# Down-projection of an encoder layer: where the lower weight parts of the odd pieces are made

## The chip, the cores and the metric

The kernel runs on one core of a Trainium2 chip. The metric is the time on the device in microseconds, the median of the timed runs. TensorE multiplies matrices out of SBUF into PSUM; VectorE, ScalarE and GpSimd work on elements; SyncE issues the plain loads from HBM, and GpSimd has a queue of transfers of its own. All transfers run on the same 16 DMA engines.

## The reference

One layer of an encoder for 256 tokens of width 2048: a mixer (forgetting attention and HGRN2), a cross attention, and a gated feed-forward block with a causal convolution, each followed by a residual and a layer norm. The change touches only the last product, `w_down`:

```
def conv_ffn(x, w_up, conv_w, conv_b, w_down):
    h = x @ w_up
    ...
    a, b = jnp.split(h, 2, axis=-1)
    return (jax.nn.silu(a) * b) @ w_down
...
ff = conv_ffn(x, ffn_up[l], conv_w[l], conv_b[l], ffn_down[l])
x = layer_norm(DEEPNORM_ALPHA * x + ff, ln3_g[l], ln3_b[l])
```

The inner width is 5632, so `w_down` is 5632 x 2048. Everything is float32.

## The kernel before

All products run in float32r, the reduced float32 of TensorE. To keep the precision each operand is split into two parts: the upper part is the value rounded to float32r, and the lower part is what the rounding left, value minus upper part. `split` (lines 76 to 78) does it with two instructions: ScalarE casts the raw tile to the upper part, VectorE subtracts the upper part from the raw tile. A product then takes three matmuls: upper activation by upper weight, upper by lower, and lower by upper (`tok_steps`, lines 256 to 258).

Weights come in pieces of 128 partitions by 2048 columns, 1 MB, one `Load` each. `Load.dma` asks SyncE for the piece into a ring of three raw tiles (`RAW_BUFS`). `Load.split` makes, for each half of 1024 columns, a tile `whi` and a tile `wlo` of 4 KB a partition, out of a pool of 38 such tiles (`unit`) that the activations and other data share. A raw tile is free again when both halves are split, and a `whi` or `wlo` tile when TensorE has used it for the last time.

The program is a list of slots. For each slot `run` first calls `advance`, which traces the loads and splits of the pieces that lie ahead (one piece of splits and three of loads, in the down-projection), then the slot's matmuls. The order on each engine's queue follows from that; how early an instruction really runs is set by the tiles that it waits for.

The down-projection is the last `block_output` (line 1071): the 2048 output columns in four chunks of 512, for each chunk 11 pieces of four k-tiles (44 in all), and for each piece `tok_steps` for both blocks of 128 tokens: 24 matmuls of 128x512. In the last chunk the last four pieces share a slot, first for the one token block and then for the other (`stagger=4`). After the second chunk `load_gb` fetches the parameters of the last norm into four more tiles of the shared pool. Behind the last matmul come the residual, the statistics, the norm and the stores.

Of the kernel before, what the change touches and what calls it, by code (L numbers as in the profile page):

```python
# [38 lines left out]
# the second norm's hand-over to the feed-forward products, by (token block, chunk, half of the chunk)  # L39
# [5 lines left out]
def tile_encoder_layer(ctx: ExitStack, tc: tile.TileContext, aps, out):  # L45
# [8 lines left out]
    def unit(shape, dtype=F32, name="u"):  # L54
        """4 KB a partition, from the pool that all larger data share."""
        return up.tile(shape, dtype, name=name, tag="u", bufs=UNITS)
# [13 lines left out]
    def hold(inst, after):  # L70
        """Keeps an instruction without operands, and its tile, from being scheduled before another."""
        tc.add_manual_dep(inst.ins, after.ins.name, mybir.DependencyInfo(
            mybir.DependencyClass.NoSync, mybir.DependencyReason.DATA), reason="hold")

# [13 lines left out]
    class Load:  # L88
        """One [128, 2048] piece of weights (or of a transposed activation)."""

        def __init__(self, src, into=None):
            self.src, self.into = src, into
# [8 lines left out]
        def split(self):  # L101
            if self.into is not None:
                split_act(self.into, r3(self.raw, 8), 0, 8)
                return
            self.halves = []
            for h in range(2):
                hi = unit([P, 1024], F32R, name="whi")
                lo = unit([P, 1024], F32R, name="wlo")
                split(hi, lo, self.raw[:, h * 1024:(h + 1) * 1024])
                self.halves.append((hi, lo))  # L110

    def fetch(dst, src):
        """A smaller load, queued behind the weights that have been asked for."""
        hold(nc.sync.dma_start(dst, src), state["load"])
# [15 lines left out]
    def background(make):  # L130
        """make() gives a generator; each slot runs its next step."""
        program.append(("bg", make))
# [9 lines left out]
    def later(fn, slots=1):  # L142
        """Traces fn some slots on, when the engines no longer wait for what it needs."""
        deferred.setdefault(state["slot"] + slots, []).append(fn)
# [9 lines left out]
    def advance(dma_to, split_to):  # L154
        """Asks for weights as far as their ring of tiles reaches, and splits them."""
        while True:
            while state["dma"] < min(dma_to, state["split"] + RAW_BUFS, len(loads)):
                loads[state["dma"]].dma(2 if state["dma"] == 2 else 1)
                state["dma"] += 1
            if state["split"] >= min(split_to, len(loads)):  # L160
                return
            loads[state["split"]].split()
            state["split"] += 1
# [29 lines left out]
    def ft_steps(acc, halves, act, k0=0, k1=KD):  # L193
        """[128 features, 512]: the two halves add up to the product for 256 tokens."""
        for k in range(k0, k1):
            hi, lo = halves[k // 8]
            cols = slice((k % 8) * P, (k % 8) * P + P)
            x = k_of(act, k)
            nc.tensor.matmul(acc, lhsT=hi[:, cols], rhs=flat(x), start=k == 0, stop=False)  # L199
            nc.tensor.matmul(acc[:, 0:S], lhsT=lo[:, cols], rhs=x[:, 0], start=False, stop=k == KD - 1)  # L200

    def block_steps(acc, halves, act, k0, k1, t):
        """One matmul alone starts the bank: the second block's first ones find it cleared."""
        ts = slice(t * P, t * P + P)
        for k in range(k0, k1):
            hi, lo = halves[k // 8]
            cols = slice((k % 8) * P, (k % 8) * P + P)
            x = k_of(act, k)
            nc.tensor.matmul(r3(acc, 2)[:, :, ts], lhsT=hi[:, cols], rhs=x[:, :, ts],  # L209
                             start=k == 0 and t == 0, stop=False)  # L210
            if t == 1:
                nc.tensor.matmul(acc[:, 0:S], lhsT=lo[:, cols], rhs=x[:, 0], start=False, stop=k == KD - 1)  # L212
# [15 lines left out]
    def products(srcs, act, evacs, steps=None):  # L228
        """Several of them, four k-tiles of each at a time. With steps, the second half of the tokens
        comes after the first, and the products with the lower parts of the weights come with it."""  # L230
        acc = []

        def body(*halves):
            acc.extend(bank("acc", "g") for _ in halves)
            for t in range(2 if steps else 1):
                for c in range(4):
                    for i, h in enumerate(halves):
                        if steps:
                            steps(t, c, i)
                            block_steps(acc[i], h, act, 4 * c, 4 * c + 4, t)  # L240
                        else:
                            ft_steps(acc[i], h, act, 4 * c, 4 * c + 4)

        def post():
            for a, evac in zip(acc, evacs):
                evac(a)

        slot(srcs, body, post, ahead=0 if steps else None)
# [11 lines left out]
    def product_tok(srcs, act, evac, order=None, stagger=0, between=None, inside=None):  # L260
        """Two [128 tokens, 512 columns] products; srcs: pieces of four k-tiles. evac(t, product)"""
# [48 lines left out]
    def keep_warm(n):  # L310
        """Products of nothing, for the clock of the tensor engine while it waits."""
        b = bank("warm", "m")
        for i in range(n):
            nc.tensor.matmul(b, lhsT=idle, rhs=idle.unsqueeze(1).broadcast_to((P, 4, P)), start=True, stop=True)

    def start():
        """The first operands, piece by piece, so that the products start early."""
# [31 lines left out]
    def parameters():  # L349
# [15 lines left out]
        # lower bound of the forget gate: softmax over a depth of one, less its first row  # L365
# [9 lines left out]
    def rsqrt(v, shape, name):  # L375
        """v ** -0.5: a guess from the exponent, then three Newton steps y <- (v y y - 3 c c) y. Each
        takes c times the root to -2 c c c times it; the guess has the c that ends at one."""
# [48 lines left out]
    def hgrn(g, d):  # L426
# [5 lines left out]
        # gates  # L432
# [13 lines left out]
        # products of gates within blocks of four: up to t (pre), after s (suf)  # L446
# [16 lines left out]
        # blocks of eight, referred to their middle  # L463
# [36 lines left out]
        def upper(t, h):  # L500
            """The upper halves of blocks of 2 h."""
            return t.rearrange("p (n i) -> p n i", i=2 * h)[:, :, h:2 * h]

        a = level(dk, dq)
        # from here on q and k carry the products within their block of h
# [54 lines left out]
        # outputs in token layout, RMS norm, gate  # L560
# [55 lines left out]
    def forget_bias():  # L616
# [9 lines left out]
        # log sigmoid  # L626
# [9 lines left out]
        # running sum over tokens  # L636
# [143 lines left out]
    def block_output(w, pieces, act, n, ln, after=None, order=None, stagger=3, inside=None, affine=True):  # L780
        """Adds act @ w to the residual; n gets the norm's parameters by token block, and its g and b."""
# [17 lines left out]
        for c in range(4):  # L799
            product_tok([w[pieces * c + i] for i in range(pieces)], act, evac(c), order,  # L800
                        stagger=stagger if c == 3 else 0, inside=inside if c == 3 else None)
            if c == 1 and affine:
                then(load_gb)

    def norm_transposed(n, act):
        """Normalises and lays all out transposed, four k-tiles a step."""
# [20 lines left out]
    def standardise(n, c, t):  # L827
        """The norm without its g and b."""
# [4 lines left out]
    def block_transposed(act, c, t):  # L833
        """Four k-tiles of a standardised token block, transposed; the steps given put g and b in, and split."""
# [24 lines left out]
    def affine(ln):  # L859
        """g and b for a residual that is standardised."""  # L860
# [14 lines left out]
    def feature_into(d, h, j):  # L875
        """Features of a head, split; d[h][j // 2][:, j % 2, part]"""
# [153 lines left out]
    def inside(left):  # L1030
        """The first token block, laid out transposed among the last products of the second."""
        if left == 1:
            transpose(0, 0, 1, 2, 3)
            advance_chunks(0, 0, 1, 0, 1, 2, 2, 3, 3)

    def norm_steps(t, c, i):
        """The second block, among the products of the first and its own."""
# [37 lines left out]
def _by_feature(w):  # L1075
    """[K, F] -> [F / 128, 128, (K / 128) * 128]"""
# [4 lines left out]
def _by_column(w):  # L1081
    """[K, C] -> [(C / 512) * (K / 512), 128, 4 * 512]"""
# [58 lines left out]
```

## Time and profile before

| | |
|---|---|
| median of 2 timed runs | 1587.66 us (1587.35 to 1587.98) |
| span of the profiled execution | 1586.8 us, at a mean granted clock of 0.997 |
| TensorE busy | 1570.9 us, 99% of the span |
| VectorE busy | 1023.3 us, 64% |
| ScalarE busy | 772.5 us, 49% |
| GpSimd busy | 10.9 us, 1% |
| moved by the DMA engines | 299.29 MB, 189 GB/s in the mean |

Only the profiled execution has a span, from its first instruction to its last; the timed runs are other executions, and their median is 0.9 us above it. Busy times overlap, so they don't add up to the span. Times of rows count from the start of the span; the matmuls of the down-projection lie between 1334 and 1574 us.

### The profile page before, as it was taken

Reading aid. Unit: us, or ns where it says so; the run is one execution under the profiler, and the core shown is the slowest. Engines: PE = TensorE matmul, PEld = TensorE weight load, DVE = VectorE, ACT = ScalarE, POOL = GpSimd, SP = SyncE. Lnnn points to the kernel's source line nnn. Section 1 sums busy time; section 2 is a strip of 40 time slices with the busy share of each in tenths; the row PEclk is TensorE's granted clock in tenths of the full one; section 3 lists DMA queues with packets and bytes.
Section 4 is the critical chain, followed back from the end, with each engine's and each line's share of the span. In section 5 each row is a group of like instructions: output and inputs, shape, how many; then the busy total and the mean of one; then the engine's idle time right before and its main releaser. Section 6 shows DMA issues by size and latency. Waiting matters only on the chain.

```text
span 1586.8 us, 20787 instructions
## 1 busy us (share of the span) xinstructions
PE 1570.9 (99%) x8324; PEld 1343.6 (85%) x8324; DVE 1023.3 (64%) x1444; ACT 772.5 (49%) x1128; POOL 10.9 (1%) x24
## 2 busy tenths in 40 slices
PE   9999999999999999999999999999999999999996
PEld 7888888888888888888889888888888888888885
DVE  6567468667664765554847976676766667454464
ACT  5453354455553344443627655565555555343350
POOL 0000000000000000000000000000000000000000
PEclk9999999999999999999999999999999999999999
DMA  8555255455446544445733754554454556556551
GB/s 306 188 229 226 108 195 184 179 219 199 157 176 223 201 178 167 159 160 185 269 129 133 267 206 164 213 185 166 179 182 164 182 177 226 196 200 212 189 208 54
DMA packets 45793, 299.29 MB, mean 189 GB/s; under 512 B 5368, under 2 KB 5760, under 8 KB 11264
## 3 DMA queue, kind: packets, MB, share of 16 engines
q1 hardware_dynamic: 45376, 296.90, 51.1%
q8 instruction: 65, 1.06, 0.3%
q0 software_dynamic: 320, 1.06, 0.2%
q14 instruction: 32, 0.26, 0.0%
HBM read 295.83 MB, written 2.11 MB: 188 GB/s over the span
## 4 chain that ended last, share of the span: by engine, by line
PE 98%; DVE 1%; DMA 0%; issue 0%; SPq 0%; DVEq 0%; ACT 0%
PE acc L199 35%; PE acc L200 18%; PE acc L256 13%; PE acc L258 13%; PE acc L257 13%; PE xs L903 1%; PE xo L933 1%; PE lev L526 1%; PE acc L209 0%; PE acc L212 0%; DMA xraw<-in_xT_dram 0%; PE fo L750 0%; PE ntr L838 0%; PE ffacc L613 0%; PE ho L568 0%; PE lev L492 0%
## 5 line engine op out<-in xcount | busy, mean ns | idle before, releaser
L199 PE MATMUL acc<-act,whi 128*128 128x512 f32 x2384 | 844.1, 399 | 1.5 <-DVE act L78 1.4
L78 DVE TENSOR_TENSOR wlo<-raw,whi 128x1024 fp32r<-128x1024 f32 (+1 forms) x540 | 642.0, 1213 | 261.6 <-ACT whi L77 232.6
L77 ACT CAST whi<-raw 128x1024 fp32r<-128x1024 f32 (+1 forms) x540 | 547.8, 1044 | 262.6 <-PE acc L257 184.1
L200 PE MATMUL acc<-act,wlo 128*128 128x256 f32 x2384 | 669.2, 281 | 0.2 <-DVE wlo L78 0.2
L199 PEld LDWEIGHTS acc<-act,whi 128*128 128x128 f32 x2384 | 448.5, 188 | 111.9 <-DVE act L78 1.7
L200 PEld LDWEIGHTS acc<-act,wlo 128*128 128x128 f32 x2384 | 450.8, 189 | 0.8 <-DVE wlo L78 0.5
L256 PE MATMUL acc<-whi,act 128*128 128x512 f32 x800 | 312.7, 391 | 0.0
L258 PE MATMUL acc<-whi,act 128*128 128x512 f32 x800 | 311.5, 389 | 0.0
L257 PE MATMUL acc<-wlo,act 128*128 128x512 f32 x800 | 311.3, 389 | 0.0
L258 PEld LDWEIGHTS acc<-whi,act 128*128 128x128 f32 x800 | 150.1, 188 | 31.6
L256 PEld LDWEIGHTS acc<-whi,act 128*128 128x128 f32 x800 | 150.2, 188 | 30.6
L257 PEld LDWEIGHTS acc<-wlo,act 128*128 128x128 f32 x800 | 150.2, 188 | 30.5
L216 ACT COPY half<-acc 128x256 f32<-128x256 f32 x144 | 53.2, 370 | 165.2 <-PE acc L200 164.7
L949 ACT ACTIVATE cy<-hbuf,convp 128x256 f32<-128x256 f32 x88 | 52.9, 601 | 45.0 <-DVE hbuf L217 44.4
L950 DVE SCALAR_TENSOR_TENSOR cy<-hbuf,convp,cy 128x256 f32<-128x256 f32 x88 | 42.4, 483 | 38.9 <-ACT cy L949 38.9
L77 ACT CAST act<-cy 128x256 fp32r<-128x256 f32 x76 | 30.9, 407 | 56.4 <-DVE cy L968 43.3
L217 DVE TENSOR_TENSOR hbuf<-acc,half 128x256 f32<-128x256 f32 x88 | 36.8, 420 | 28.8 <-ACT half L216 28.7
L256 PE MATMUL acc<-whi,mixT 128*128 128x512 f32 x128 | 50.0, 390 | 0.0
L258 PE MATMUL acc<-whi,mixT 128*128 128x512 f32 x128 | 49.8, 389 | 0.0
L257 PE MATMUL acc<-wlo,mixT 128*128 128x512 f32 x128 | 49.8, 389 | 0.0
L760 DVE SCALAR_TENSOR_TENSOR res<-res,acc 128x512 f32<-128x512 f32 x24 | 16.4, 684 | 48.2 <-PE acc L258 48.2
L78 DVE TENSOR_TENSOR act<-cy,act 128x256 fp32r<-128x256 f32 x76 | 32.0, 421 | 20.6 <-ACT act L77 20.6
(204 smaller groups left out, 735.9 us busy)
## 6 DMA issues: line engine op xcount, KB each, us to landing
raw<-in_up_dram SPq DMA_DIRECT2D x88, 1024.0 KB, 4.8
raw<-in_down_dram SPq DMA_DIRECT2D x44, 1024.0 KB, 4.8
raw<-in_w_ws_dram SPq DMA_DIRECT2D x29, 1024.0 KB, 4.9
raw<-in_w_xs_dram SPq DMA_DIRECT2D x24, 1024.0 KB, 5.0
raw<-in_xk_dram SPq DMA_DIRECT2D x16, 1024.0 KB, 4.8
raw<-in_w_out_dram SPq DMA_DIRECT2D x16, 1024.0 KB, 4.9
raw<-in_xv_dram SPq DMA_DIRECT2D x16, 1024.0 KB, 4.8
raw<-in_xq_dram SPq DMA_DIRECT2D x16, 1024.0 KB, 4.8
```

What stands on the lines that cost most here:

```text
L77: nc.scalar.copy(hi, src)
L78: engine.tensor_tensor(lo, src, hi.bitcast(F32), op=ALU.subtract)
L199: nc.tensor.matmul(acc, lhsT=hi[:, cols], rhs=flat(x), start=k == 0, stop=False)
L200: nc.tensor.matmul(acc[:, 0:S], lhsT=lo[:, cols], rhs=x[:, 0], start=False, stop=k == KD - 1)
L216: nc.scalar.copy(half, acc[:, S:2 * S])
L217: nc.vector.tensor_tensor(dst, acc[:, 0:S], half, op=ALU.add)
L256: nc.tensor.matmul(acc[t], lhsT=x[:, 0, ts], rhs=hi[:, cols], start=first and j == 0, stop=False)
L257: nc.tensor.matmul(acc[t], lhsT=x[:, 0, ts], rhs=lo[:, cols], start=False, stop=False)
L258: nc.tensor.matmul(acc[t], lhsT=x[:, 1, ts], rhs=hi[:, cols], start=False, stop=last and j == 3)
L760: nc.vector.scalar_tensor_tensor(z, in0=z, scalar=ALPHA, in1=acc, op0=ALU.mult, op1=ALU.add)
L949: nc.scalar.activation(y, h[:, 2:S + 2], AF.Identity, bias=convp[:, 3, f:f + 1], scale=convp[:, 2, f:f + 1])
L950: nc.vector.scalar_tensor_tensor(y, in0=h[:, 1:S + 1], scalar=convp[:, 1, f:f + 1], in1=y, op0=ALU.mult, op1=ALU.add)
```

## The change

In the down-projection alone (the only product with 11 pieces a chunk), the pieces at odd places of a chunk, 1, 3, 5, 7 and 9, get their lower parts in another way. ScalarE casts the upper part as before, then writes its negative into the tile of the lower part, and a transfer on GpSimd's queue adds the same weights, read from HBM once more, to that tile. VectorE does nothing for these pieces. The raw tile is read by ScalarE alone. The result is the same: minus the upper part, plus the value. The even pieces are as before. (Other lines of the diff only drop comments.)

```
         def __init__(self, src, into=None, added=False):
             self.src, self.into, self.added = src, into, added
...
             for h in range(2):
                 hi = unit([P, 1024], F32R, name="whi")
                 lo = unit([P, 1024], F32R, name="wlo")
-                split(hi, lo, self.raw[:, h * 1024:(h + 1) * 1024])
+                cols = slice(h * 1024, (h + 1) * 1024)
+                if self.added:
+                    nc.scalar.copy(hi, self.raw[:, cols])
+                    nc.scalar.activation(lo, hi.bitcast(F32), AF.Copy, scale=-1.0)
+                    nc.gpsimd.dma_start(lo, self.src[:, cols], accum_op=ALU.add)
+                else:
+                    split(hi, lo, self.raw[:, cols])
                 self.halves.append((hi, lo))
...
         for c in range(4):
-            product_tok([w[pieces * c + i] for i in range(pieces)], act, evac(c), order,
+            added = lambda i: pieces == 11 and i % 2 == 1
+            product_tok([Load(w[pieces * c + i], added=added(i)) for i in range(pieces)], act, evac(c), order,
                         stagger=stagger if c == 3 else 0, inside=inside if c == 3 else None)
```

## Rows read from the trace of the kernel before

**Rows 1.** The page, its first part: busy time, share of the span, instructions.

```profile
span 1586.8 us, 20787 instructions
...
PE 1570.9 (99%) x8324; PEld 1343.6 (85%) x8324; DVE 1023.3 (64%) x1444; ACT 772.5 (49%) x1128; POOL 10.9 (1%) x24
```

**Rows 2.** The page, the chain that ended last, by engine.

```profile
PE 98%; DVE 1%; DMA 0%; issue 0%; SPq 0%; DVEq 0%; ACT 0%
```

**Rows 3.** Waits, 1332 to 1574 us: who for whom, total us, times, longest.

```profile
ACT whi L77 <- PE acc L257: 124.4, 70, 8.5
DVE wlo L78 <- ACT whi L77: 97.0, 37, 8.3
DVE res L760 <- PE acc L258: 17.5, 4, 15.6
```

**Rows 4.** Windows: busy us of each engine, clock, DMA share, GB/s.

```profile
11.00:18.00 7.00, 7.00 (x38) 6.09 (x37) 6.11 (x10) 5.33 (x9) 0.00 (x0) 0.90 0.97 365
1332.00:1557.00 225.00, 225.00 (x998) 186.37 (x997) 112.81 (x105) 89.06 (x89) 0.00 (x0) 1.00 0.55 200
```

**Rows 5.** Lines by form, 1332 to 1574 us: busy us, mean ns, idle before.

```profile
L256 PE MATMUL acc<-whi,act 128*128 128x512 f32 x352 | 137.0, 389 | 0.0
...
L257 PE MATMUL acc<-wlo,act 128*128 128x512 f32 x352 | 136.9, 389 | 0.0
L78 DVE TENSOR_TENSOR wlo<-raw,whi 128x1024 fp32r<-128x1024 f32 x86 | 104.2, 1224 | 100.8 <-ACT whi L77 97.0
```

**Rows 6.** Timeline of TensorE: first and last matmul (start, us).

```profile
1334.46 0.40 PE L256 MATMUL acc<-whi,act 128*128 128x512 f32 x1
...
1573.66 0.39 PE L258 MATMUL acc<-whi,act 128*128 128x512 f32 x1
```

**Rows 7.** Timeline of ScalarE: casts of weights; in brackets the idle time before.

```profile
1329.72 1.05 ACT L77 CAST whi<-raw 128x1024 fp32r<-128x1024 f32 x1
...
1331.18 2.94 ACT L77 CAST whi<-raw 128x1024 fp32r<-128x1024 f32 x3
...
1338.58 1.06 ACT L77 CAST whi<-raw 128x1024 fp32r<-128x1024 f32 x1 [0.78 <-PE acc L257]
...
1436.50 1.05 ACT L77 CAST whi<-raw 128x1024 fp32r<-128x1024 f32 x1 [3.02 <-PE acc L257]
...
1447.38 1.05 ACT L77 CAST whi<-raw 128x1024 fp32r<-128x1024 f32 x1 [8.46 <-PE acc L257]
...
1512.66 1.05 ACT L77 CAST whi<-raw 128x1024 fp32r<-128x1024 f32 x1 [3.02 <-PE acc L257]
...
1539.86 3.10 ACT L77 CAST whi<-raw 128x1024 fp32r<-128x1024 f32 x3 [2.48 <-PE acc L257]
1545.30 1.05 ACT L77 CAST whi<-raw 128x1024 fp32r<-128x1024 f32 x1 [2.34 <-PE acc L257]
```

**Rows 8.** Waits of SyncE's queue, 1332 to 1574 us.

```profile
SPq L99 <- DVE wlo L78: 181.2, 38, 6.8
```

**Rows 9.** Instructions of line 435, ScalarE: ns minimum, median, maximum.

```profile
L435 ACT ACT_TABLE_LOAD  x2: 1283/1283/1283, 99.7 to 230.0; - x2
L435 ACT ACTIVATE hk<-hz x2: 1058/1060/1062, 101.0 to 231.3; 128x1024 f32<-128x1024 f32 x2
```

**Rows 10.** Timeline of GpSimd: its 512 KB transfers and its last instruction.

```profile
381.20 1.09 POOL L650 DMA_DIRECT2D ncb<-cscr  x2 [2.18 <-DMA cscr<-ffc]
...
836.63 1.43 POOL L78 TENSOR_TENSOR act<-xf,act 128x256 fp32r<-128x256 f32 x2 [0.62 <-POOL act L78]
```

**Rows 11.** DMA view, 1332 to 1557 us: total, and loads with us to landing.

```profile
DMA packets 6474, 45.11 MB, mean 200 GB/s; under 512 B 720, under 2 KB 720, under 8 KB 1232
...
raw<-in_down_dram SPq DMA_DIRECT2D x40, 1024.0 KB, 4.8
```

**Rows 12.** DMA view, 378 to 388 us: GpSimd's queue (share of that window).

```profile
q0 software_dynamic: 320, 1.06, 32.3%
...
ncb<-cscr POOLq DMA_DIRECT2D x2, 512.0 KB, 4.5
```

More of the change, by code (lines that the diff above doesn't have):

```diff
@@ L88, in tile_encoder_layer, with __init__ @@
     class Load:
-        def __init__(self, src, into=None):
-            self.src, self.into = src, into
+        def __init__(self, src, into=None, added=False):
+            self.src, self.into, self.added = src, into, added
         def dma(self, pieces=1):
```

## The prediction

> **What bounds the kernel now.** I read the page first: TensorE is busy for 1570.9 us of a span of 1586.8 us [rows 1], and the chain that ended last runs 98% through it [rows 2]. So a change counts only if it shortens TensorE's own work or makes TensorE wait. Next come the waits of the stretch of the down-projection, 1332 to 1574 us: ScalarE waits for TensorE, VectorE for ScalarE and TensorE, and no row has TensorE waiting for anything [rows 3]. In the windows TensorE is busy for all 225 us between 1332 and 1557 at a granted clock of 1.00, while VectorE is busy for 113 us, ScalarE for 89, GpSimd for none, and the 16 DMA engines for a share of 0.55 [rows 4]. The lines give 352 matmuls of each of three kinds and no idle time before any of them [rows 5]. They begin at 1334.46, and the last starts at 1573.66 and takes a further 0.23 us of issue by the spacing of the starts [rows 6]: 239.4 us for 1056, so 0.227 us each, and 24 x 0.227 = 5.44 us for a piece of weights. This pace is TensorE's own; the split of the weights runs beside it. The profiled execution has a span of 1586.8 us, and the median of the timed runs is 1587.7, so 0.9 us lies around the span.
>
> **How far ahead the split runs.** The question is how long a lower part may take. There are 44 pieces, so 88 casts on ScalarE. Counted back from the last, at 1545.30, the cast at 1512.66 is the first half of piece 35 (counted from 0), and at one piece each 5.44 us the one at 1447.38 is piece 23, the one at 1436.50 piece 22, the one at 1338.58 piece 4 and the one at 1329.72 piece 1 [rows 7]. TensorE comes to piece n at 1334.46 + 5.44 n: to piece 22 at 1454.1, so the cast leads by 17.6 us, and to piece 23 at 1459.6 and piece 35 at 1524.9, where it leads by 12.2 us. The lead falls where `load_gb` takes four of the shared tiles for the last norm. These casts wait for TensorE [rows 7]: tiles, not ScalarE or the loads, set the lead.
>
> **The change part by part.** *Removed from VectorE:* odd places in a chunk of 11 are five pieces, times four chunks, times two halves: 40 subtractions of 1.224 us [rows 5], 49 us. VectorE idles 100.8 us before these subtractions already and TensorE waits for none of them, so this gives back nothing.
>
> *Added on ScalarE:* 40 negated copies. The nearest row is an activation of 128x1024 with a scale of -1, 1.060 us [rows 9]: 42 us, and ScalarE goes from 89 to 131 us of 225. If the function needs a table, 1.28 us once [rows 9]. Queued behind a negated copy is the cast of the next half; it comes about 1 us later and still has some 10 us of lead. At the seam with the up-projection the last evacuations also queue behind it; their products are used only at the end of the first chunk. Cost 0.
>
> *Moved past queues:* SyncE's loads wait for VectorE's subtraction to give back the ring of raw tiles, 181 us over 38 waits [rows 8]. For odd pieces the second cast gives it back, about 1 us sooner. No later work than that is late there: cost 0. GpSimd's queue has been empty since 838 us; its two earlier transfers of 512 KB took 0.55 us each to issue [rows 10], so 40 take 22 us of 225, in order, and only adding transfers stand behind one that waits.
>
> *Added in time to landing:* after the change the first matmul with a lower part waits for a landing, with the whole in-order queue of TensorE behind it. For piece 23, the tightest kind: cast 1447.38 to 1448.4, negated by 1449.5, second half cast by 1450.5 and negated by 1451.6. The nearest row of the transfer is the plain 512 KB from GpSimd's queue, 4.5 us from issue to landing [rows 12]: the lower parts land at 1454.0 and 1456.1. They are wanted at 1459.8 and 1461.2, so 5 us is spare. The first changed piece has less: with the two extra copies and one evacuation its second half is negated by 1334.4 and lands by 1339, wanted at 1341.5. Cost 0, and up to some 2 us once if landing takes that much longer.
>
> *Added on the DMA engines:* this is the dear part and no row shows an adding transfer. From 1332 to 1557 the engines moved 45.11 MB [rows 11] in a share of 0.55 of 225 us, 124 us [rows 4]; the other 101 us are room. Almost all odd pieces fall into it, so 40 transfers have 101 / 40 = 2.5 us of all 16 engines each. Bounds: below, the rate of these loads, 124 us / 45.11 MB x 0.524 MB = 1.44 us, as if adding were free. Above, 4.5 us, the landing time of the plain transfer [rows 12] taken as if all of it occupied the engines and nothing overlapped. A gain is excluded, since 20 MB more is moved. I take 1.6 us: GpSimd's queue took 32.3% of 10 us for its 1.06 MB [rows 12], half of which is one such transfer, and it is the only row of that queue. Then 40 x 1.6 = 64 us, the share goes from 0.55 to 0.84 and everything fits; the engines have run at 0.97, moving 365 GB/s, in the load burst at the start [rows 4]. Loss 0. Beyond 2.5 us the excess turns into waiting of TensorE, about 40 a - 101 us for a price of a us.
>
> The Trainium skill speaks against that choice: "Collectives: The Full Stack", section "The bandwidth ceiling: the fold count and why AG ≠ RS ≠ AR", states that a ReduceScatter ran at half the rate of an AllGather, not because the addition costs cycles but because it needs two source reads. No run here shows it so far; by it the sum would be that of the second rival.
>
> **Sum.** -0 for VectorE, +0 for ScalarE, SyncE and GpSimd, +0 on the DMA engines, the last 12.9 us after TensorE's end untouched: 1587.7 + 0 to 1, rounded to 1588 us. About 2% (31.8 us) is what a measurement of this kernel tells from no change.
>
> **Rivals.** *1. DMA engines saturate and the stage becomes bound by them (slower).* Place: 1332 to 1557. Price as above: it decides from 2.5 us per adding transfer, and passes 2% from (101 + 31.8) / 40 = 3.3 us. At 4.5 us it costs 40 x 4.5 - 101 = 79 us, so 1667 us. For it: the room is only 1.6 times the plain price, the addition must read its destination besides, and float32 becomes float32r on the way. Against: 12 to 17 us of lead and a plain transfer of the same queue at 1.6 us.
>
> *2. Two reads for one write.* The engines take in the weights and the negated copy, 2 x 1.44 = 2.9 us, or 3.2 us by the queue's own row. (This is the mechanism of the page of the Trainium skill named above.) Then 40 x 2.9 - 101 = 15 us, or 28 us: 1603 to 1616 us, short of 2%. For it: the destination has to be read. Against: only one of the two reads comes from HBM, and the writes, which the loads also have, are not doubled; at 2.5 us or below nothing is lost.
>
> *3. Relief of VectorE pays, or the change doesn't do what it says.* If the lower parts were what TensorE stands behind, 40 subtractions would give up to 49 us; but there is no idle time before these matmuls [rows 5], so the most that I can find is nothing. If the condition met no piece, the time would be 1587.7; eleven pieces is what the down-projection alone has, so it meets twenty.
>
> **How the numbers follow.** Hidden, 1586 to 1591 us: 0.50. Two reads or another price between 2.5 and 3.3 us, 1591 to 1619 us: 0.25. Saturated beyond 3.3 us, over 1619 us: 0.23. Faster over 2%: 0.02. So within 2% is 0.75. The range starts at 1585; at the top 1640 is a price of (52 + 101) / 40 = 3.8 us, and I leave some 0.16 to what lies between that and 4.5 us and a little above, and 0.02 to a gain.
>
> **What would show it.** Right: in the profile after, 48 subtractions left on VectorE in the down-projection, 40 more activations near 1.06 us, 40 issues on GpSimd near 0.55 us, a DMA share of about 0.84 in the stretch, landings of 5 to 8 us, and no idle time before the matmuls of line 257's kind. Rival 1: a DMA share near 1, landings growing from piece to piece beyond 10 us, and TensorE idle before the first lower-part matmul of odd pieces, released by a DMA. Rival 2: the same with a few us for each chunk. What would make me wrong most easily is the price of the adding transfer, then a different order of the instructions on ScalarE.

## The result and the profile after

The changed kernel takes 1609.15 us (median of 2 runs, 1606.21 to 1612.10) against 1587.66 us: a ratio of 1.0134, 95% interval 1.0114 to 1.0153. That is 21.5 us more, within the 2% that were called no change and within the range, but 21 us above the 1588 us of my sum. The profiled execution took 1606.2 us with a span of 1604.1. The other one, 1612.1 us, has no trace, so what follows explains the 17.3 us of the two spans.

The page of the changed kernel, its first part, one queue of its third part, and the chain that ended last:

```profile
span 1604.1 us, 20877 instructions
...
PE 1575.2 (98%) x8324; PEld 1345.9 (84%) x8324; DVE 976.0 (61%) x1404; ACT 812.4 (51%) x1168; POOL 45.4 (3%) x64
...
q0 software_dynamic: 6080, 22.03, 7.3%
...
PE 58%; issue 37%; DMA 3%; POOL 1%; DVE 1%; ACT 0%; SPq 0%; DVEq 0%; POOLq 0%
```

VectorE lost 47 us and ScalarE gained 40, close to the 49 and 42 costed, and neither matters, as a run below shows. New against [rows 2] is that the chain leaves TensorE for transfers. Most of the 37% of "issue" (time in which an engine waited for nothing that the profile shows) is one stretch of 494 us, 839 to 1334 us: followed back through GpSimd's transfers, the chain comes to a time in which GpSimd had nothing to do. It is no loss, since TensorE was busy then, for 494.5 of 495 us. The waits of the changed kernel, 1332 to 1595 us (who for whom, total us, times, longest), have a row that [rows 3] lacks:

```profile
PEld acc L263 <- DMA wlo<-in_down_dram: 15.6, 8, 3.7
PE acc L263 <- DMA wlo<-in_down_dram: 12.2, 8, 3.3
```

Its lines by form in the same stretch answer to [rows 5]: line 263 is the lower-part matmul, 112 the negated copy, 113 the adding transfer.

```profile
L263 PE MATMUL acc<-wlo,act 128*128 128x512 f32 x352 | 138.7, 394 | 12.2 <-DMA wlo<-in_down_dram 12.2
...
L78 DVE TENSOR_TENSOR wlo<-raw,whi 128x1024 fp32r<-128x1024 f32 x46 | 56.0, 1224 | 146.6 <-ACT whi L77 144.5
...
L112 ACT ACTIVATE wlo<-whi 128x1024 fp32r<-128x1024 f32 x40 | 42.4, 1059 | 1.1
...
L113 POOL DMA_DIRECT2D wlo<-in_down_dram x40 | 34.5, 863 | 689.6 <-DVE cy L959 494.5 <-ACT wlo L112 192.6 <-PE acc L206 1.3
```

The DMA view of 1332 to 1574 us (packets, MB, share of the engines in the window; then KB each and median us to landing) and the window that answers to [rows 4]:

```profile
q1 hardware_dynamic: 6480, 45.09, 48.5%
q0 software_dynamic: 5760, 20.97, 47.2%
...
raw<-in_down_dram SPq DMA_DIRECT2D x40, 1024.0 KB, 9.5
wlo<-in_down_dram POOLq DMA_DIRECT2D x40, 512.0 KB, 10.9
```

```profile
1332.00:1557.00 225.00, 212.76 (x928) 173.55 (x927) 64.33 (x64) 123.87 (x124) 32.80 (x38) 0.99 0.98 282
```

The packets of an adding transfer took 47.2% x 242 / 40 = 2.86 us of the 16 engines, not 1.6, and landed after 10.9 us, not 4.5. The share in the window is 0.98, so the obvious reading is that the DMA engines are full.

Where the time went is seen in TensorE. Between the first matmul of the stage, at 1335.67, and the start of the last, at 1590.93, lie 255.3 us, against 239.2 [rows 6]: 16.1 us more (the other 1.2 us of the span arose before the stage). TensorE waited eight times: twice for the first changed piece (1342 to 1347), five times 0.6 to 1.4 us between 1466 and 1534, and once 3.3 us at 1547. No wait fell into the second chunk, though the engines were as busy there (a share of 0.98 from 1400 to 1460 us, 0.97 in the next 60). A typical late one, the timeline of TensorE (idle time in brackets), with the second half's transfer of that piece, issued at 1480.0:

```profile
1490.62 0.39 PE L262 MATMUL acc<-whi,act 128*128 128x512 f32 x1
1492.44 0.50 PE L263 MATMUL acc<-wlo,act 128*128 128x512 f32 x1 [1.43 <-DMA wlo<-in_down_dram]
```

```profile
L113 POOL DMA_DIRECT2D wlo<-in_down_dram x1: 862/862/862, 1477.9 to 1477.9; - x1
...
L113 POOL DMA_DIRECT2D wlo<-in_down_dram x1: 862/862/862, 1480.0 to 1480.0; - x1
...
DMA to landing us min/median/max: 12.4/12.4/12.4
```

1480.0 + 12.4 = 1492.4: the matmul starts when the second half lands. The first half was in time.

### The profile page after: what moved, and what is told of

The parts are those of the page before. It is cut to its first block, busy times and chain, and to the rows that moved or that the text cites. A ratio compares the mean times of both kernels' runs of the same rounds, so it can differ in the third digit from the quotient of the medians.

```text
span 1604.1 us, 20877 instructions
## 1 busy us (share of the span) xinstructions
PE 1575.2 (98%) x8324; PEld 1345.9 (84%) x8324; DVE 976.0 (61%) x1404; ACT 812.4 (51%) x1168; POOL 45.4 (3%) x64
## 4 chain that ended last, share of the span: by engine, by line
PE 58%; issue 37%; DMA 3%; POOL 1%; DVE 1%; ACT 0%; SPq 0%; DVEq 0%; POOLq 0%
PE acc L205 15%; PE acc L263 10%; PE acc L262 10%; PE acc L264 10%; PE acc L206 8%; DMA wlo<-in_down_dram 2%; POOL wlo L113 1%; PE xs L910 1%; PE xo L940 1%; PE lev L532 1%; DMA xraw<-in_xT_dram 0%; PE fo L756 0%; PE ffacc L619 0%; PE lev L498 0%; PE ho L574 0%
## 5 line engine op out<-in xcount | busy, mean ns | idle before, releaser
L78 DVE TENSOR_TENSOR wlo<-raw,whi 128x1024 fp32r<-128x1024 f32 (+1 forms) x500 | 594.1, 1213 | 307.9 <-ACT whi L77 280.5
L77 ACT CAST whi<-raw 128x1024 fp32r<-128x1024 f32 (+1 forms) x500 | 506.1, 1042 | 179.6 <-PE acc L263 98.6
L263 PE MATMUL acc<-wlo,act 128*128 128x512 f32 x800 | 313.2, 392 | 12.2 <-DMA wlo<-in_down_dram 12.2
L111 ACT CAST whi<-raw 128x1024 fp32r<-128x1024 f32 x40 | 41.6, 1041 | 59.4 <-PE acc L263 53.9
L223 DVE TENSOR_TENSOR hbuf<-acc,half 128x256 f32<-128x256 f32 x88 | 36.9, 420 | 28.8 <-ACT half L222 28.7
L113 POOL DMA_DIRECT2D wlo<-in_down_dram x40 | 34.5, 863 | 689.6 <-DVE cy L959 494.5
## 6 DMA issues: line engine op xcount, KB each, us to landing
wlo<-in_down_dram POOLq DMA_DIRECT2D x40, 512.0 KB, 10.9
```

What stands on the lines that cost most here:

```text
L77: nc.scalar.copy(hi, src)
L78: engine.tensor_tensor(lo, src, hi.bitcast(F32), op=ALU.subtract)
L111: nc.scalar.copy(hi, self.raw[:, cols])
L113: nc.gpsimd.dma_start(lo, self.src[:, cols], accum_op=ALU.add)
L263: nc.tensor.matmul(acc[t], lhsT=x[:, 0, ts], rhs=lo[:, cols], start=False, stop=False)
```

## The experiments

Theory A: an adding transfer occupies the DMA engines twice as long as a copy, the engines are full, and TensorE follows them. Theory B: the engines still keep pace, but one adding transfer takes 9 us or more to land beside the loads, which is more than the lead of the split leaves it in places. For B the limits are these: in the third chunk the transfers are issued 2.4 and 4.5 us after the piece's first cast (for the piece above, this cast and the issues at 1477.9 and 1480.0):

```profile
1475.50 1.05 ACT L111 CAST whi<-raw 128x1024 fp32r<-128x1024 f32 x1 [3.02 <-PE acc L263]
```

By the lead of 12.2 us of the kernel before, the halves are wanted 12.4 and 13.8 us after the cast, so landings may take 10.0 and 9.3 us. With the longer lead of the first two chunks it is 5.4 us more. A wait of TensorE between the cast and the use adds to the limit: in the piece above the wait for the changed piece before it (that matmul starts at 1479.8) lies in between, the second half had 10.9 us, and its 12.4 us were late by about 1.5. Theory C: GpSimd's queue, or the second stream of weights from HBM, is slow whatever it carries.

**A plain copy instead of the addition.**

```
-                    nc.gpsimd.dma_start(lo, self.src[:, cols], accum_op=ALU.add)
+                    nc.gpsimd.dma_start(lo, self.src[:, cols])
```

> The 40 transfers no longer add: a plain copy of the weights over the negated parts, on the same queue, with the same bytes from HBM and the same waits (the lower parts are then wrong). Theory A, the addition doubles what the 16 DMA engines have to take in (2.9 us a transfer, 1.4 to 1.6 us for a copy): landing falls from 10.9 us to about 5 to 6 us, TensorE waits for none, the time is 1588 to 1592 us. Theory C, GpSimd's queue or the second stream of weights from HBM is what is slow, whatever the transfer does: landing stays near 10 us and the time near 1609 us.

Measured: 1588.67 us, ratio 1.0002 (0.9992 to 1.0011). DMA view, 1332 to 1574 us, and the window:

```profile
q0 software_dynamic: 5760, 20.97, 28.8%
...
wlo<-in_down_dram POOLq DMA_DIRECT2D x40, 512.0 KB, 6.5
```

```profile
1332.00:1557.00 225.00, 225.00 (x998) 186.40 (x997) 66.30 (x65) 128.98 (x129) 21.15 (x40) 1.00 0.84 294
```

The copy takes 28.8% x 242 / 40 = 1.74 us of the engines, the share is 0.84 as I had worked out, and TensorE waits for nothing. Theory C is out: bytes, queue and the change of the number format are the same; the addition is what costs. The recorded expectation names A and C only; the outcome fits B as well.

**Fewer adding transfers.**

```
-            added = lambda i: pieces == 11 and i % 2 == 1
+            added = lambda i: pieces == 11 and i in (1, 5, 9)
```

> Only places 1, 5 and 9 of each chunk are changed: 24 adding transfers and not 40. Theory A, engine time: 24 x 2.9 = 70 us fit into the room of 101 us, so all waits vanish save the one at the first piece (up to 4 us): 1588 to 1593 us. Theory B, an adding transfer takes 11 us to land by itself, however idle the engines are: landing stays near 11 us and the late pieces, with a lead of 12.2 us, still wait 1 to 2 us each: 1597 to 1602 us.

Measured: 1598.49 us, ratio 1.0065 (1.0050 to 1.0080). The share is 0.84, the same as with plain copies, and yet TensorE waits six times:

```profile
1332.00:1557.00 225.00, 218.65 (x961) 179.17 (x961) 83.56 (x79) 112.53 (x112) 20.73 (x24) 1.00 0.84 253
```

```profile
PE acc L263 <- DMA wlo<-in_down_dram: 6.3, 6, 2.6
```

The two transfers of one piece of the third chunk (landing minimum, median, maximum), and TensorE:

```profile
L113 POOL DMA_DIRECT2D wlo<-in_down_dram x2: 862/862/862, 1453.7 to 1455.7; - x2
...
DMA to landing us min/median/max: 9.3/9.7/10.1
```

```profile
1465.91 0.50 PE L263 MATMUL acc<-wlo,act 128*128 128x512 f32 x1 [0.64 <-DMA wlo<-in_down_dram]
```

The second half lands at 1455.7 + 10.1 = 1465.8, 0.8 us over its limit of 9.3, and TensorE waits 0.64 us. That is B in one piece, at a share that leaves room. The time is in B's range, though the four late waits are 0.6 to 0.8 us and not 1 to 2. The long landing is partly the loads beside it: the last two transfers of this kernel, issued from 1552.8 us when the loads were over (the last is issued at 1544.5), landed sooner. The last two of the kernel with plain copies, issued 7 us and more after its last load, were faster still, in the second fence:

```profile
L113 POOL DMA_DIRECT2D wlo<-in_down_dram x2: 862/862/862, 1552.8 to 1554.8; - x2
...
DMA to landing us min/median/max: 6.3/6.5/6.8
```

```profile
L113 POOL DMA_DIRECT2D wlo<-in_down_dram x2: 527/528/528, 1543.6 to 1545.7; - x2
...
DMA to landing us min/median/max: 4.3/4.5/4.7
```

So B as it was recorded for this run, 11 us however idle the engines are, does not hold; the landing is that long only in company.

**A longer lead in the third chunk.**

```
-            if c == 1 and affine:
+            if c == (2 if pieces == 11 else 1) and affine:
                 then(load_gb)
```

> All 40 adding transfers, but the last norm's parameters are fetched a chunk later, so the third chunk keeps a lead of 17.6 us instead of 12.2. Theory A in its strict form (the engines lag steadily behind): the waits of the third chunk only move later, the time stays at 1605 to 1609 us. Theory B, or A with the engines just able to keep pace: the four waits of the third chunk (4.5 us together) vanish, 1602 to 1605 us.

Measured: 1601.38 us, ratio 1.0082 (1.0063 to 1.0100), just below the figure for B. The four waits of the third chunk are gone; the two at the seam stay, and two for one piece of the last chunk. The total is helped less than the waits: of the 12.8 us that the stage lost, 7.4 are late starts of the waiting matmuls and 4.6 are matmuls at a lower clock (last section), against 13.5 and 1.4 of 16.1 in the changed kernel. Waits of TensorE in the stage:

```profile
PE acc L263 <- DMA wlo<-in_down_dram: 6.8, 4, 2.9
```

**More adding transfers.**

```
-            added = lambda i: pieces == 11 and i % 2 == 1
+            added = lambda i: pieces == 11 and i % 3 != 0
```

> Places 1, 2, 4, 5, 7, 8 and 10 of each chunk are changed: 56 adding transfers. Theory A: 56 x 2.9 - 101 = 61 us above 1588, so 1645 to 1652 us, with a DMA share near 1 and waits in every chunk. Theory B: a wait of some 1 to 2 us at each late changed piece and few in the first two chunks, 1615 to 1625 us.

Measured: 1629.51 us, ratio 1.0254 (1.0236 to 1.0272), between the two forecasts. With 56 transfers there are waits in every chunk, landings of 12.5 us in the median, and a share above one; 7 of the 14 waits fall into the first two chunks, where B expected few, so neither theory holds alone. The time is also not waiting alone: of the 38.4 us that the stage lost in the profiled execution, 26.8 are late starts of the waiting matmuls and 9.6 are matmuls at the lower clock, which neither forecast had. The waits and the window, with a granted clock of 0.96:

```profile
PE acc L263 <- DMA wlo<-in_down_dram: 24.5, 14, 3.4
```

```profile
1332.00:1557.00 225.00, 204.33 (x858) 164.25 (x858) 43.12 (x46) 124.69 (x126) 40.58 (x47) 0.96 1.02 286
```

**The same transfers, wanted later.** Within a piece the products with lower parts come last. (In the other products that use `tok_steps` the order of the second and the third matmul changes with it; the stage began at 1333.5 us, not later than before.)

```
-            nc.tensor.matmul(acc[t], lhsT=x[:, 0, ts], rhs=hi[:, cols], start=first and j == 0, stop=False)
-            nc.tensor.matmul(acc[t], lhsT=x[:, 0, ts], rhs=lo[:, cols], start=False, stop=False)
-            nc.tensor.matmul(acc[t], lhsT=x[:, 1, ts], rhs=hi[:, cols], start=False, stop=last and j == 3)
+            if part != 1:
+                nc.tensor.matmul(acc[t], lhsT=x[:, 0, ts], rhs=hi[:, cols], start=first and j == 0, stop=False)
+                nc.tensor.matmul(acc[t], lhsT=x[:, 1, ts], rhs=hi[:, cols], start=False, stop=False)
+            if part != 0:
+                nc.tensor.matmul(acc[t], lhsT=x[:, 0, ts], rhs=lo[:, cols], start=False, stop=last and j == 3)
...
-                for t in range(2):
-                    tok_steps(acc, halves, act, order[i], t, i == 0, i == n - 1)
+                for part in ((0, 1) if n == 11 else (None,)):
+                    for t in range(2):
+                        tok_steps(acc, halves, act, order[i], t, i == 0, i == n - 1, part)
```

> All 40 adding transfers, but within a piece the 16 products with upper weight parts come first and the 8 with lower parts last (in the shared slot at the end, 8 and then 4 for each block of tokens). The work of TensorE and of the DMA engines is the same; the first lower part is wanted 3.6 us into a piece and not 0.2. Theory B (landing of about 9 and 10 us and more against a lead of 12.2 us): the waits of 1 to 1.5 us of the third chunk vanish and those of 3 to 4 us shrink to 1 us at most: 1589 to 1595 us. Theory A (the DMA engines are full and TensorE follows them): the sum of the waits stays, 1601 to 1609 us.

Measured: 1590.65 us, ratio 1.0018 (1.0008 to 1.0027). This tells the theories apart. The window, the lower-part matmuls (line 266 here, 1332 to 1574 us) and the landing over all 40:

```profile
1332.00:1557.00 225.00, 223.41 (x988) 184.77 (x987) 64.85 (x63) 128.98 (x128) 34.20 (x40) 1.00 1.02 292
```

```profile
L266 PE MATMUL acc<-wlo,act 128*128 128x512 f32 x349 | 87.2, 389 | 1.6 <-DMA wlo<-in_down_dram 1.6
```

```profile
DMA to landing us min/median/max: 6.2/10.2/14.7
```

The engines do all the work of the changed kernel, in less time, at a share of 1.02, and the landings are nearly as long (10.2 us in the median against 10.9). What was changed is the moment at which a lower part is wanted, and 2.5 us of loss are left of 21.5.

**ScalarE's part alone.**

```
-                    nc.gpsimd.dma_start(lo, self.src[:, cols], accum_op=ALU.add)
```

> The transfer is left out; ScalarE casts and negates as in the changed kernel, VectorE does nothing for the odd pieces (the lower parts are then minus the upper ones). This is the part of ScalarE and VectorE alone. Every theory that puts the loss on the transfer: 1588 to 1589 us. If the queue of ScalarE had a share in it: above 1590 us.

Measured: 1588.13 us, ratio 1.0000 (0.9990 to 1.0009). The negated copies and VectorE's relief are worth nothing, in either direction.

**Adding from SBUF.**

```
-                    nc.gpsimd.dma_start(lo, self.src[:, cols], accum_op=ALU.add)
+                    nc.gpsimd.dma_start(lo, self.raw[:, cols], accum_op=ALU.add)
```

> The transfers add the raw tile in SBUF and not the weights from HBM: 20 MB less from HBM, the same two reads for each write. If the second read from HBM is what makes the landing long: landing 5 to 6 us, no waits for it, 1588 to 1592 us. If adding itself occupies the engines: landing stays at 9 to 12 us and the DMA share near 1. The raw tile is then held about 10 us longer, so loads and casts wait as well: 1605 to 1640 us.

Measured: 1625.77 us, ratio 1.0241 (1.0224 to 1.0258), in the range that I gave for tiles held longer. Half of the landings still take 8.6 us or more without the second read of HBM, between the two values forecast, and the share is 0.91. TensorE waits 14 times, 20.6 us in sum, and the raw tiles come back late, as the waits of SyncE's queue and of ScalarE show (1332 to 1600 us):

```profile
SPq L99 <- DMA wlo<-raw: 196.7, 22, 14.2
```

```profile
ACT whi L77 <- DMA raw<-in_down_dram: 69.8, 17, 11.5
```

How much of a landing is the read from HBM can't be told from this run, since the loads beside the transfers moved too.

**Fewer, with the lead and without the seam.**

```
-            added = lambda i: pieces == 11 and i % 2 == 1
+            added = lambda i: pieces == 11 and i in (1, 5, 9) and (c, i) != (0, 1)
...
-            if c == 1 and affine:
+            if c == (2 if pieces == 11 else 1) and affine:
```

> Places 1, 5 and 9, without place 1 of the first chunk, and the last norm's parameters a chunk later: 22 adding transfers, all but the last chunk's with a lead of 17.6 us. Theory B with the seam as a case of its own: of the waits of the kernel with 24 (3.7 us at the seam, four of 0.7) one or two in the last chunk stay: 1588.5 to 1590.5 us. If part of its 9.9 us was not waiting of TensorE: 1591 to 1596 us.

Measured: 1589.25 us, ratio 1.0009 (1.0000 to 1.0018); one wait of 0.8 us in the last chunk. Set beside the kernel of 24 transfers, which lost 9.9 us, it shows that all but about 1 us of that loss went with the seam and the leads.

**The seam alone.**

```
-            added = lambda i: pieces == 11 and i % 2 == 1
+            added = lambda i: pieces == 11 and i % 2 == 1 and (c, i) != (0, 1)
```

> As the changed kernel, but place 1 of the first chunk keeps its subtraction on VectorE: 38 adding transfers. If the waits at the seam come from that piece's short lead (about 10 us for its first half, less the extra work of ScalarE there), its 3.7 us of waiting go and the five later ones stay: 1602 to 1606 us. If the second changed piece takes over the seam's wait: 1606 to 1610 us.

Measured: 1600.87 us, ratio 1.0084 (1.0069 to 1.0099), a little below the first forecast. That is 8.3 us less than the changed kernel took, over twice the 3.7 us of the seam's waits, so the later waits changed too. TensorE still waits 7.2 us in four places, but not as before: the third chunk has two waits and not four, one of them of 2.4 us. Why the later waits fell differently, these runs don't settle.

**All three mends together**, with 38 adding transfers: `(c, i) != (0, 1)`, the norm's parameters a chunk later, and lower-part products last, as in the diffs above.

> 38 adding transfers (without place 1 of the first chunk), the last norm's parameters a chunk later, and the lower-part products last in a piece. Theory B: no wait of TensorE is left, 1588 to 1589.5 us, at a DMA share near 1. It should not be below the kernel before, since the pace of TensorE is the same. Theory A: above 1592 us.

Measured: 1588.51 us, ratio 1.0003 (0.9993 to 1.0013). Window and lower-part matmuls:

```profile
1332.00:1557.00 225.00, 225.00 (x996) 186.32 (x995) 66.12 (x65) 127.68 (x125) 32.89 (x38) 1.00 0.99 287
```

```profile
L266 PE MATMUL acc<-wlo,act 128*128 128x512 f32 x352 | 87.6, 389 | 0.0
```

TensorE waits for nothing at a DMA share of 0.99. No version was faster than the kernel before. I expect none by this route: from the first to the last start the stage takes 239.2 us here as in the kernel before, which is TensorE's own pace.

## Why the prediction was right and where it was off

*What bounds the kernel* held: with the transfer left out the time is the old one to within 0.1%, so relief of VectorE gives nothing.

*ScalarE, SyncE and GpSimd at 0* held. The negated copy took 1.059 us (1.060 costed); no table was loaded. An issue on GpSimd took 0.86 us and not 0.55, which hid as well.

*Time to landing: this is the step that failed.* It took the 4.5 us of a plain transfer from another stage and found 5 us to spare. Beside the loads of this stage a plain copy landed after 6.5 us in the median; an adding transfer took 8.5 to 10.3 us in the third chunk of the kernel with 24, where the share was 0.84, and 10.9 us in the median of the changed kernel, up to 16.5, against limits of 10.0 and 9.3 us in the third chunk. Why the addition makes a landing longer stays open. The mechanism that I named there, the in-order queue of TensorE behind one landing, is what happened; its price was less than half of the real one, and the "2 us once" at the seam was 3.7. In the profiled execution the eight starts came 13.5 us late in sum and 1.4 us more went to the clock (below), of the 16.1 us; most of the rest is the matmul behind each waiting one, which started 0.34 us after it and not 0.23.

*Engine time: the value was too low and the rule built on it too strict.* I took 1.6 us and kept 2.9 as the second rival. Measured was 2.86 us of packet time (30.4% x 242 / 24 = 3.07 in the kernel with 24 transfers), 2.86 / 1.74 = 1.64 times the copy of the same queue. The rule of the Trainium skill that I set against my choice ("Collectives: The Full Stack", "The bandwidth ceiling: the fold count and why AG ≠ RS ≠ AR": an addition needs two source reads, which halved the rate there) points the same way, but this case gives 1.64 and not 2. And what I made of it, that the excess 40 a - 101 turns into waiting, is not what the runs show: it gives 13 us at that price, and the kernels with lower parts last have the same engine work (40 and 38 transfers) and lose 2.5 us, or 0.4 with all mends. So the measured time lies between the second rival's 1603 and 1616 us by another way than its own, and that it lies within my range is luck: I had widened the range for the price on the engines and not for the landing. A share near 1 was no proof of full engines here: it came out at 1.02 too, more than 16 engines have, so packet times overlap in it, and 2.86 us is a sum of packet times and not shown to be occupancy. Of the signs that I named for the first rival, the share and the idle TensorE came, but the landings didn't grow from piece to piece: the two issued at 1502.9 and 1505.0 us landed after 9.3 and 10.1 us. With 56 transfers TensorE waited in the chunks with the long lead too. Whether the engines have no room left in the mean there or the transfers of two pieces in a row are too many at once, these runs don't settle.

*The span:* I put 0.9 us around it. In the profiled executions timed here it is about 2 us (1606.2 against 1604.1), which doesn't change the comparison.

## What to carry to other kernels

When work moves from an engine to a transfer, compare two times: how long the transfer takes to land beside the traffic that will be there, and how long the operand's tile is free before its first use. Price an adding transfer by more than a plain one of its size (here 2.86 us of packet time and not 1.74), and its landing by a transfer that had company. If it comes late, first look whether the consumer can use that operand last: reordering 24 matmuls within a piece did more here than taking 40% of the transfers away.

## What the runs showed of the hardware

After its longest wait TensorE ran at half speed for some 2.7 us. Timeline of TensorE in the changed kernel, and the window 1548 to 1550 us (granted clock third from the right):

```profile
1547.76 0.80 PE L263 MATMUL acc<-wlo,act 128*128 128x512 f32 x1 [3.33 <-DMA wlo<-in_down_dram]
1548.35 0.63 PE L264 MATMUL acc<-whi,act 128*128 128x512 f32 x1
1548.77 0.63 PE L262 MATMUL acc<-whi,act 128*128 128x512 f32 x1
...
1550.79 0.39 PE L264 MATMUL acc<-whi,act 128*128 128x512 f32 x1
```

```profile
1548.00:1550.00 2.00, 2.00 (x5) 1.59 (x6) 0.00 (x0) 1.97 (x2) 0.00 (x0) 0.50 1.02 326
```

A granted clock of 0.50 is the lower of its two levels, 1.2 GHz: the matmuls start 0.43 us apart and not 0.227. The seven starts after the wait cost 1.4 us by that. After the waits of 0.6 to 2.7 us in the same execution the spacing was back at 0.23 us one matmul later. The length of the wait alone doesn't decide, though: in the run without the seam's transfers a wait of 2.4 us was followed by the lower clock (timeline, and the window 1476 to 1478 us).

```profile
1475.15 0.79 PE L263 MATMUL acc<-wlo,act 128*128 128x512 f32 x1 [2.42 <-DMA wlo<-in_down_dram]
```

```profile
1476.00:1478.00 2.00, 2.00 (x6) 1.52 (x6) 0.00 (x0) 0.00 (x0) 0.00 (x0) 0.50 1.05 301
```
